# Layer 1's first feed-forward matrix by seven block products instead of eight, in chunks 2 to 7

## The chip, the cores and the metric

The kernel runs on one core of a Trainium2 chip. The metric is the device time of one execution in microseconds: 1711.4 us before the change (median of three runs, 1711.36 to 1712.46). Engines: PE = TensorE matmul, PEld = its weight load, DVE = VectorE, ACT = ScalarE, POOL = GpSimd, SP = SyncE, which issues nearly all DMAs here.

## The reference

Two trunk layers over 640 tokens (512 latent, 128 context) of width 1024; each is a mixer (attention and convolution) and then a feed-forward part. Only that of layer 1, the last one, is touched:

```
def trunk_layer(x, cvec, lw, layer, ctx):
    ...
    h = rmsnorm(x, lw['g_ff']) * (1.0 + sc2) + sh2
    x = x + g2 * (jnp.square(jax.nn.relu(h @ lw['w_ff1'])) @ lw['w_ff2'])
    return x, new_ctx
```

`w_ff1` is 1024 x 4096 and `w_ff2` 4096 x 1024, all float32. After the last layer comes a final RMS norm.

## The kernel before

Activations lie transposed: features on the 128 partitions, the 640 tokens along the free dimension. So `h` is 8 tiles of 128 x 640, and the hidden layer is 32 tiles of 128 x 640, worked on in 8 chunks of 4 tiles. The token range is cut in two, `HALF = ((0, 384), (384, 640))`, so that a piece fits one PSUM bank of 512 columns. There are eight banks, used in turn (`g()`).

Every float32 operand is kept as a high part (rounded by a cast to fp32r on ScalarE) and a low part (source minus high part): `split`. A product is then three matmuls, high x high, high x low, low x high (`mm3`, lines 245 to 247), accumulated in one bank. For weights the low part is computed by GpSimd, with a few exceptions in the mixer.

Weights arrive in granules of 128 x 1024 float32 (512 KB) by DMA on SP's queue into three raw buffers (`w_dma`), are split in blocks of 512 columns into one of four slots (`w_cut`, `split`), and a slot is free again when the last matmul that reads it is done (`w_done`). One granule of `w_ff1` is one hidden tile (8 k-tiles of 128 x 128); one of `w_ff2` is 512 rows x 256 columns (4 k-tiles, two output tiles).

`ff(l)` is the loop. Chunk 0 is started together with the norm (`ff1_start`). Then for chunk c = 1 to 7 and q = 0 to 3: `ff1(c, q)` makes hidden tile q of chunk c (48 matmuls: 24 of 384 columns, 24 of 256), and `ff2(c - 1, q)` adds two output tiles' share of the chunk before (again 24 and 24). `ff2_end` does the last chunk's second matrix. After each `ff1` half, `ff1_after` makes the hidden values: relu (ACT, from PSUM), square to the high part (ACT), square on DVE, low part by a subtraction on DVE. After each `ff2` piece, `resid` adds it to `x` on DVE. In layer 0 the same loop also runs background jobs (`bg`); in layer 1 it has none.

A scheduler puts each engine's instructions in an order by program order, a priority and its own estimate of when each is ready; within an engine they then run strictly in that order. The hidden tiles live in two buffers that alternate by chunk (`hid`). The memory of the mixer's tiles (`e`, `mla`, `c`, `rope`, `edge`) is part of the arena `fa` for the whole program.

Of the kernel before, what the change touches and what calls it, by code (L numbers as in the profile page):

```python
# [9 lines left out]
F32 = mybir.dt.float32  # L10
# [24 lines left out]
def _addresses(sizes, base=0):  # L35
# [42 lines left out]
KINDS = ("D", "D")  # L78
ROWS = (1,1,0,0)
END = object()  # L80
PROGRAM = "Sa0 ma0 | T2 ev2 xa0 Sb0 mb0 xb0 sc1 | PV3 oc3 |".split()


class Builder:
    def __init__(self, tc, sb, ps, d):
        self.tc, self.nc, self.d = tc, tc.nc, d
        self.fa = sb.tile([128, F_SIZE // 4], F32, name="fa")
        self.ra = sb.tile([128, R_SIZE // 4], F32R, name="ra")
        self.gb = [ps.tile([128, 512], F32, name=f"g{i}") for i in range(2)]
# [24 lines left out]
        self.right = self.squares = None  # L114
        self.last_square = False
        self.w_split = self.w_load = 0
        self.ng = L * NGRAN

    def _view(self, arena, at, shape):
        n = int(np.prod(shape))  # L120
# [5 lines left out]
        return v  # L126

    def F(self, name, off, *shape):
        return self._view(self.fa, F_AT[name] + off, shape)

    def R(self, name, off, *shape):
# [84 lines left out]
            self.w_load += 1  # L216

    def w_cut(self):
        while self.w_split < min(self.w_load, self.ng):
            n = self.w_split  # L220
            i = self.w_slot(n)
            if self.held[i] or (i > 1 and self.we is None):
                return
            self.held[i] = True
            raw = self.w_raw(n)
            hi, lo = self.w_hl(n)
            for j, s in enumerate((slice(0, 512), slice(512, 1024))):
                self.split(hi[:, s], lo[:, s], raw[:, s], self.nc.vector if n < 4 and CUT[n * 2 + j] == "D" or n > 3 and j and i > 1 and n % NGRAN < NMIX + 4 else None)
            self.w_split += 1
            self.w_dma()  # L230

    def w_get(self, c):
        n = self.w_n
# [918 lines left out]
    def ff2_piece(self, l, c, wv, m, mm, h):  # L1152
        t0, t1 = HALF[h]
        ps = self.g()
        for k in range(4):
            hi, lo = self.hid(c, k)
            cols = slice(mm * 128, mm * 128 + 128)
            self.mm3(ps[:, 0:t1 - t0], (wv[0][:, k, cols], wv[1][:, k, cols]), (hi[:, t0:t1], lo[:, t0:t1]), k == 0, k == 3)
        return ps

    def ff2(self, l, c, q):
        wv = self.w_get(256)
        for h in range(2):
            for mm in range(2):
                m = 2 * q + mm
                ps = self.ff2_piece(l, c, wv, m, mm, h)
                if h == 1 and mm == 1:
                    self.w_done()
                self.resid(l, G2, m, h, ps)
            self.tick(1200)  # L1170

    def ff2_end(self, l, c, chain):
        ws = [self.w_get(256) for _ in range(4)]
        for h in range(2):
            for q in range(4):
                for mm in range(2):
                    m = 2 * q + mm
                    ps = self.ff2_piece(l, c, ws[q], m, mm, h)
                    if h == 1 and mm == 1:
                        self.w_done()  # L1180
# [25 lines left out]
    def start(self):  # L1206
# [123 lines left out]
        for _ in range(3):  # L1330
            self.w_dma()
        self.chain(self.mod_rows(0, (G1, SC2, SH2, G2)))
        nc.sync.dma_start(self.F("rope", 0, 1152), d["cst"][:, 0:1152])
# [145 lines left out]
    def ff(self, l):  # L1479
        nc = self.nc  # L1480
        self.ring = self.banks
        self.junk = self.F("e", 0, 1024)
        ring = [self.F("e", 4096, 1024), self.F("e", 8192, 1024), self.F("mla", 0, 1024)]
        self.bg = []
        self.ff1_start(l)
        if l + 1 < L:
            self.bg = self.mod_jobs(l + 1, range(6), ring, BGP[4])
        for c in range(1, 8):
# [5 lines left out]
        self.norm_at("mla", 6144)  # L1494
        if l + 1 < L:
            self.mod_gain(l + 1, 0)
            self.lead = self.norm(l + 1, 0, 0)
# [48 lines left out]
    def run(self):  # L1546
        with (self.tc.manual_schedule(engines={getattr(mybir.EngineType, e) for e in MAN}) if MAN else contextlib.nullcontext()):
            self.o_tile("s", F32)
            self.swap("s", "we")
            for l in range(L):  # L1550
                with self.tc.tile_pool(name=f"at{l}", bufs=1) as pool:
                    self.at = pool.tile([128, A_SIZE // 4], F32, name=f"at{l}")
                    self.mix(l)
                with self.tc.tile_pool(name=f"hd{l}", bufs=1) as pool:
                    self.hd = pool.tile([128, 4480], F32R, name=f"hd{l}")
                    self.ff(l)
            self.right.__exit__(None, None, None)
            self.under.__exit__(None, None, None)
# [45 lines left out]
def _layout(a):  # L1604
# [5 lines left out]
    for l in range(L):  # L1610
# [103 lines left out]
```

## Time and profile before

| | us |
|---|---|
| median of 3 runs | 1711.4 |
| the profiled execution, whole | 1712.74 |
| its span, first to last instruction | 1710.7 |
| PE busy / DVE / ACT / POOL | 1633.3 / 1051.2 / 728.2 / 659.3 |

The profiled execution is 1.3 us over the median; 2.0 us of it lie outside the span. Times below are microseconds from the span's start. In layer 1's feed-forward the granules follow one another every 7.03 us: chunk 1 starts at 1278.2, chunk 2 at 1334.4, `ff2_end` at 1671.9.

### The profile page before, as it was taken

The numbers are of one execution on the slowest core, as the hardware profiler recorded it, in microseconds if no ns is written. First come the engines' busy times: TensorE is split into PE (matmuls) and PEld (weight loads), VectorE is DVE, ScalarE is ACT, GpSimd is POOL, SyncE is SP. The second block draws the span as 40 slices with busy tenths as digits, with TensorE's granted clock in tenths as the row PEclk, the third lists the DMA queues.
The fourth block names the chain that finished last, engine by engine and source line by source line (L and its number), as shares of the span: only waits on it lengthen the run. The fifth ranks groups of instructions, "written<-read, shape, count | busy, mean of one in ns | idle before, by whom it ended". The sixth has DMA issues, their size and how long they took to land. (4 is left out here: it accounts for less than half of the span.)

```text
span 1710.7 us, 29286 instructions
## 1 busy us (share of the span) xinstructions
PE 1633.3 (95%) x11416; PEld 1531.2 (90%) x11416; DVE 1051.2 (61%) x2064; ACT 728.2 (43%) x1617; POOL 659.3 (39%) x527
## 2 busy tenths in 40 slices
PE   7989999999899999999999899999999999999997
PEld 4867988878899999999999888887789999999997
DVE  4791438867788787885377943886773333333335
ACT  4322576755622222233343257676553323332222
POOL 0242543414444444544324364341443333333330
PEclk7998999999999999999999999999999999999999
DMA  9465333302244454443222233330112222222221
GB/s 358 157 227 173 100 101 98 88 21 79 71 151 157 151 159 152 157 150 99 75 71 72 65 95 101 86 87 21 50 57 92 74 75 75 75 74 75 75 62 62
DMA packets 62330, 178.27 MB, mean 104 GB/s; under 512 B 8656, under 2 KB 20048, under 8 KB 62192
## 3 DMA queue, kind: packets, MB, share of 16 engines
q1 hardware_dynamic: 61984, 176.14, 33.7%
q8 instruction: 89, 1.46, 0.4%
q14 instruction: 49, 0.40, 0.1%
q0 software_dynamic: 64, 0.14, 0.0%
q10 hardware_dynamic: 144, 0.13, 0.0%
HBM read 158.52 MB, written 3.83 MB: 95 GB/s over the span
## 5 line engine op out<-in xcount | busy, mean ns | idle before, releaser
L194 POOL TENSOR_TENSOR ra<-fa,ra 128x512 fp32r<-128x512 f32 (+1 forms) x239 | 353.4, 1494 | 501.8 <-ACT ra L193 481.9
L194 POOL TENSOR_TENSOR we<-fa,we 128x512 fp32r<-128x512 f32 x126 | 185.7, 1485 | 261.3 <-ACT we L193 239.6
L1098 DVE TENSOR_TENSOR fr<-fr 128x384 f32<-128x384 f32 (+1 forms) x128 | 102.2, 800 | 281.5 <-ACT or L1097 153.5
L193 ACT CAST ra<-fa 128x512 fp32r<-128x512 f32 (+1 forms) x240 | 147.2, 622 | 252.7 <-PE s L246 152.7
L245 PE MATMUL s<-ra 128*128 128x256 f32 (+2 forms) x704 | 218.7, 311 | 2.4 <-DVE fa L1386 2.1
L246 PE MATMUL s<-ra 128*128 128x256 f32 (+2 forms) x704 | 217.8, 309 | 0.0
L247 PE MATMUL s<-ra 128*128 128x256 f32 (+2 forms) x704 | 217.4, 309 | 0.0
L393 DVE SCALAR_TENSOR_TENSOR fa<-s,fa 128x128 f32<-128x128 f32 (+1 forms) x312 | 121.9, 427 | 73.8 <-PE s L247 73.7
L193 ACT CAST we<-fa 128x512 fp32r<-128x512 f32 x132 | 81.5, 620 | 180.5 <-PE s L246 132.2
L302 DVE CUSTOM_DVE_ANT_0 fa<-fa 128x1024 f32<-128x1024 f32 x96 | 153.4, 1598 | 0.1
L245 PEld LDWEIGHTS s<-ra 128*128 128x128 f32 x704 | 134.2, 191 | 8.4 <-issue 4.0
L393 DVE SCALAR_TENSOR_TENSOR fa<-g,fa 128x128 f32<-128x128 f32 (+1 forms) x264 | 109.2, 443 | 44.5 <-PE g L247 43.8
L246 PEld LDWEIGHTS s<-ra 128*128 128x128 f32 x704 | 134.1, 190 | 2.4 <-issue 2.3
L247 PEld LDWEIGHTS s<-ra 128*128 128x128 f32 x704 | 134.0, 190 | 0.2 <-issue 0.2
L247 PE MATMUL g<-ra 128*128 128x256 f32 (+2 forms) x404 | 123.7, 306 | 9.1 <-POOL ra L194 9.1
L245 PE MATMUL g<-ra 128*128 128x256 f32 (+2 forms) x404 | 128.1, 317 | 0.7 <-ACT fa L656 0.4
L424 DVE SCALAR_TENSOR_TENSOR fa<-fa 128x670 f32<-128x670 f32 x120 | 127.0, 1123 | 0.4
L246 PE MATMUL g<-ra 128*128 128x256 f32 (+2 forms) x404 | 123.4, 306 | 0.0
L245 PE MATMUL g<-or,ra 128*128 128x384 f32 (+1 forms) x328 | 112.8, 344 | 4.8 <-DVE or L194 4.4
L246 PE MATMUL s<-ra,we 128*128 128x256 f32 (+1 forms) x360 | 112.2, 312 | 4.6 <-DVE ra L371 4.6
L245 PE MATMUL s<-ra,we 128*128 128x256 f32 (+1 forms) x360 | 110.6, 309 | 4.2 <-DVE fa L393 2.3
L247 PE MATMUL s<-ra,we 128*128 128x256 f32 (+1 forms) x360 | 110.5, 307 | 0.0
(294 smaller groups left out, 4425.1 us busy)
## 6 DMA issues: line engine op xcount, KB each, us to landing
fa<-in_wg SPq DMA_DIRECT2D x187, 512.0 KB, 3.7
fa<-in_wmod SPq DMA_DIRECT2D x68, 512.0 KB, 4.3
at<-in_wmod SPq DMA_DIRECT2D x25, 512.0 KB, 7.2
ra<-ra SPq DMA_DIRECT2D x64, 96.0 KB, 2.5
ra<-ra SPq DMA_DIRECT2D x64, 80.0 KB, 2.8
fa<-in_nab SPq DMA_DIRECT2D x24, 192.0 KB, 4.0
fa<-in_xT SPq DMA_DIRECT2D x8, 320.0 KB, 6.7
os<-in_wmod SPq DMA_DIRECT2D x3, 512.0 KB, 10.2
```

The costliest lines, as they stand in the source:

```text
L193: nc.scalar.copy(hi, src)
L194: (lo_eng or nc.gpsimd).tensor_tensor(out=lo, in0=src, in1=hi.bitcast(F32), op=ALU.subtract)
L245: nc.tensor.matmul(out, a[0], b[0], start=start, stop=False)
L246: nc.tensor.matmul(out, a[0], b[1], start=False, stop=False)
L247: nc.tensor.matmul(out, a[1], b[0], start=False, stop=stop)
L302: self.nc.vector.tensor_tensor_reduce(out=self.junk, in0=slot, in1=self.cb[:, v], scale=1.0, scalar=0.0, op0=ALU.mult, op1=ALU.add, accum_ ...
L393: self.mark = nc.vector.scalar_tensor_tensor(out=xs, in0=ps[:, a - t0:b - t0], scalar=self.mod(l, v, which)[:, m:m + 1], in1=xs, op0=ALU.m ...
L424: nc.vector.scalar_tensor_tensor(out=y, in0=g[:, j:j + 670], scalar=dwh[:, c, j:j + 1], in1=y, op0=ALU.mult, op1=ALU.add)
L1098: nc.vector.tensor_tensor(out=r, in0=r, in1=r, op=ALU.mult)
```

## The change

For chunks 2 to 7 of layer 1, two hidden tiles are made at a time (`ff1_pair`). Their matrix product, 256 outputs by 1024 inputs by 640 tokens, is cut in two by two blocks: two output tiles, two halves of the inputs (4 k-tiles each), two halves of the tokens (`TH` = 320). Instead of eight block products seven are made (Strassen's method in Winograd's form), each of 4 k-tiles x 3 = 12 matmuls of 320 columns. Some of the seven take sums of blocks as operands, and their results are combined by additions:

- weights: `unit_jobs` makes three sums and one difference of 512 columns per pair on DVE, in `ts` or in place in the raw buffers; seven blocks are split instead of four. Two raw granules are taken up together, and their buffers go back together, after the seventh block.
- tokens: `t_jobs` makes T1, T2, T3 (in the new tile `tt`), each in 4 k-tiles, high and low part, as background jobs in chunk 1, and T4 in place of the quarter of `h` that is used no more, after the last `ff1` of chunk 1. They are used by all 12 pairs.
- results: one copy on ACT and seven additions on DVE per pair, each from a PSUM bank and an SBUF buffer; then relu, square and low part on 320 columns, four times (`hid_out`).

The four slots become eight units of one 512-column block each (`unit`, `unit_cut`, `unit_done`); second-matrix granules take two units. From chunk 2 on the order is: pair, `ff2`, `ff2`, pair, `ff2`, `ff2`. To make room, the mixer's tiles move to an arena of their own (`fm`), which is given back before the feed-forward of layer 1.

```
@@ class Builder
+WINO = NGRAN * (L - 1) + NMIX + 12
+TH = T // 2
...
     def w_cut(self):
+        if self.jobs:
+            self.unit_cut()
         while self.w_split < min(self.w_load, self.ng):
             n = self.w_split
+            if n >= WINO:
+                return self.unit_cut()
...
+    def unit_jobs(self, n):
...
+        a11, a12, a21, a22 = raw[:, 0:512], raw[:, 512:1024], nxt[:, 0:512], nxt[:, 512:1024]
+        s3, s2 = self.ts[:, 0:512], self.ts[:, 512:1024]
...
+        def sums():
+            sub(s3, a11, a21)
+            sub(a21, a21, a22, ALU.add)
+            return sub(s2, a21, a11)
+
+        def both():
+            self.w_dma()
+            self.w_dma()
+        return [lambda: a11, sums, lambda: a12, lambda: s3, lambda: a21, lambda: a22, lambda: sub(a12, a12, s2), both]
+
+    def unit_cut(self):
+        while True:
...
+            u = self.un % 8
+            if self.busy[u] or self.held[u // 2]:
+                return
+            src = self.jobs.pop(0)()
+            hi, lo = self.unit(u)
+            self.split(hi, lo, src)
...
+    def t_jobs(self):
...
+        def t1(k):
+            x, y = part(0, 1, k), part(0, 0, k)
+            hold[k] = combine((x[0], y[0]), (x[1], ALU.add), (y[1], ALU.subtract))
+            put(0, k, hold[k])
+
+        def t2(k):
+            x = part(1, 1, k)
+            put(1, k, combine((x[0], hold[k]), (x[1], ALU.add)))
+
+        def t3(k):
+            x, y = part(1, 1, k), part(0, 1, k)
+            put(2, k, combine((x[0], y[0]), (x[1], ALU.add), (y[1], ALU.subtract)))
+
+        def t4(k):
+            x, y = part(1, 0, k), [a[:, k].bitcast(F32) for a in self.t_view(1)]
+            put(3, k, combine((x[0], y[0]), (x[1], ALU.add), (y[1], ALU.subtract)))
+        return [(1500, lambda f=f, k=k: f(k), 0) for k in range(4) for f in (t1, t2, t3)], [lambda k=k: t4(k) for k in range(4)]
...
+    def ff1_pair(self, c, m):
...
+        nc.scalar.copy(s1, product(self.quarter(0, 0)))
+        add(u2, product(self.t_view(1)), s1)
+        result(product(self.quarter(1, 0)), s1, m, 0)
+        add(u3, product(self.t_view(2)), u2)
+        p5 = product(self.t_view(0))
+        result(p5, u3, m + 1, 1)
+        add(u4, p5, u2)
+        result(product(self.quarter(0, 1)), u3, m + 1, 0)
+        result(product(self.quarter(1, 1)), u4, m, 1)
...
     def ff(self, l):
...
+        if last:
+            self.bg, fourth = self.t_jobs()
         for c in range(1, 8):
             for q in range(4):
+                if last and c > 1:
+                    if q % 2 == 0:
+                        self.ff1_pair(c, q)
+                        self.ff2(l, c - 1, q)
+                        self.ff2(l, c - 1, q + 1)
+                    continue
                 self.ff1(c, q)
+                if last and q == 3:
+                    self.drain()
+                    for job in fourth:
+                        job()
                 self.ff2(l, c - 1, q)
```

How the change moves instructions, at the two places that matter below. First DVE, at the end of chunk 1. Before (L1098 and L1099 make the low part of a hidden tile, L393 adds an output piece to `x`):

```order
L1098 TENSOR_TENSOR fr_10931<-fr_10931 128x384
L1099 TENSOR_TENSOR or<-fr_10931,or 128x384
L1098 TENSOR_TENSOR fr_10931<-fr_10931 128x256
L1099 TENSOR_TENSOR or<-fr_10931,or 128x256
L393 SCALAR_TENSOR_TENSOR fa<-s_65,fa 128x384
L393 SCALAR_TENSOR_TENSOR fa<-s_66,fa 128x384
L393 SCALAR_TENSOR_TENSOR fa<-s_67,fa 128x128 x2
L393 SCALAR_TENSOR_TENSOR fa<-g_63,fa 128x128 x2
```

Now, in the same place on DVE (L1259 and L1261 combine T sums, L201 is the low part of a split: written to `tt` for T1 to T3, to `ra` for T4; L465 is `resid`; L1313 the first addition of the first pair):

```order
L201 TENSOR_TENSOR tt_10997<-fa,tt_10997 128x320
L1261 TENSOR_TENSOR fa<-fa,tt_10997 128x320
L1259 TENSOR_TENSOR fa<-ra,tt_10997 128x320
L465 SCALAR_TENSOR_TENSOR fa<-s_70,fa 128x384
L201 TENSOR_TENSOR ra<-fa,ra 128x320
L1261 TENSOR_TENSOR fa<-fa,ra 128x320
L465 SCALAR_TENSOR_TENSOR fa<-s_71,fa 128x128
L1261 TENSOR_TENSOR fa<-fa,tt_10997 128x320
L465 SCALAR_TENSOR_TENSOR fa<-s_71,fa 128x128
L465 SCALAR_TENSOR_TENSOR fa<-g_67,fa 128x128 x2
L201 TENSOR_TENSOR ra<-fa,ra 128x320
L1313 TENSOR_TENSOR fa<-s_69,fa 128x320
```

The T sums stand between the residual additions of chunk 1's last `ff2`, and the low part of T4's last k-tile is the last of them, just ahead of the first pair's additions.

Second ACT, at the start of chunk 2. Before (L193 is the cast of a weight block, L1096 and L1097 the relu and square of hidden tile 3 of chunk 1 and of tile 0 of chunk 2):

```order
L193 CAST ra<-fa 128x512 x2
L1096 ACTIVATE fr_10931<-s_67 128x256
L1097 ACTIVATE or<-fr_10931 128x256
L193 CAST ra<-fa 128x512 x2
L1096 ACTIVATE fr_10931<-g_64 128x384
L1097 ACTIVATE hd_10991<-fr_10931 128x384
```

Now (L200 is the cast of a split: 512 columns are a weight unit, 320 columns a T tile, in `tt` T3, in `ra` T4; L1168 and L1169 are the relu and square, L1323 the copy of the first product):

```order
L1168 ACTIVATE fr_10935<-s_71 128x256
L1169 ACTIVATE or<-fr_10935 128x256
L200 CAST ra<-fa 128x320
L200 CAST tt_10997<-fa 128x320
L200 CAST ra<-fa 128x512
L200 CAST ra<-fa 128x320
L200 CAST ra<-fa 128x512
L200 CAST we_10933<-fa 128x512
L200 CAST ra<-fa 128x320
L1323 COPY fa<-g_68 128x320
```

The last three casts of T4 now stand among the casts of the weight units, and each of these waits for PE to leave the unit.

## Rows read from the trace of the kernel before

**Rows 1.** The page: busy time, share of span and instructions of each engine.

```profile
PE 1633.3 (95%) x11416; PEld 1531.2 (90%) x11416; DVE 1051.2 (61%) x2064; ACT 728.2 (43%) x1617; POOL 659.3 (39%) x527
```

**Rows 2.** Windows: busy us (instructions) of each engine, granted clock; chunks 1, 2, 7.

```profile
1278.18:1334.40 56.22, 56.22 (x386) 56.22 (x385) 22.14 (x43) 18.58 (x38) 22.46 (x18) 1.00 0.28 88
1334.40:1390.66 56.26, 56.26 (x386) 56.26 (x385) 19.15 (x41) 16.80 (x33) 20.67 (x17) 1.00 0.25 76
...
1615.70:1671.90 56.20, 56.20 (x386) 56.20 (x385) 19.11 (x40) 16.74 (x33) 20.61 (x17) 1.00 0.20 57
```

**Rows 3.** Timeline of PE: start, length, engine, line; one granule of `w_ff1`.

```profile
1404.44 0.34 PE L245 MATMUL s<-ra 128*128 128x384 f32 x1
...
1408.61 0.28 PE L245 MATMUL g<-ra 128*128 128x256 f32 x1
...
1411.48 0.34 PE L245 MATMUL g<-hd,ra 128*128 128x384 f32 x1
```

**Rows 4.** Timeline of PE, at 172 us: matmuls of 288 columns.

```profile
171.77 0.29 PE L246 MATMUL s<-ra 128*128 128x288 f32 x1
...
172.30 0.30 PE L247 MATMUL s<-ra 128*128 128x288 f32 x1
```

**Rows 5.** Groups by form, 1300 to 1690 us: busy us, mean ns, idle before.

```profile
L393 DVE SCALAR_TENSOR_TENSOR fa<-s,fa 128x384 f32<-128x384 f32 x46 | 28.3, 615 | 22.4 <-PE s L247 22.4
L393 DVE SCALAR_TENSOR_TENSOR fa<-s,fa 128x128 f32<-128x128 f32 x80 | 24.4, 347 | 32.8 <-PE s L247 32.8
L1099 DVE TENSOR_TENSOR or<-fr,or 128x384 fp32r<-128x384 f32 x14 | 7.8, 557 | 0.5
L1099 DVE TENSOR_TENSOR or<-fr,or 128x256 fp32r<-128x256 f32 x15 | 6.4, 427 | 0.5
L193 ACT CAST we<-fa 128x512 fp32r<-128x512 f32 x52 | 32.3, 620 | 80.5 <-PE s L246 79.1
L1096 ACT ACTIVATE fr<-s 128x384 f32<-128x384 f32 x20 | 9.8, 492 | 72.2 <-PE s L247 72.2
L1097 ACT ACTIVATE or<-fr 128x384 fp32r<-128x384 f32 x14 | 7.3, 524 | 0.4
L194 POOL TENSOR_TENSOR we<-fa,we 128x512 fp32r<-128x512 f32 x52 | 67.2, 1303 | 115.5 <-ACT we L193 113.9
```

**Rows 6.** Groups by form, whole span: a 512-column subtraction on DVE.

```profile
L194 DVE TENSOR_TENSOR wes<-fa,wes 128x512 fp32r<-128x512 f32 x4 | 2.5, 684 | 0.0
```

**Rows 7.** Timeline of DVE and POOL at 1278 to 1285 us.

```profile
1278.17 3.95 POOL L194 TENSOR_TENSOR ra<-fa,ra 128x512 fp32r<-128x512 f32 x3 [1.50 <-ACT ra L193]
...
1279.76 1.23 DVE L1098 TENSOR_TENSOR fr<-fr 128x256 f32<-128x256 f32 x1 [2.34 <-ACT hd L1097]
...
1281.02 1.39 DVE L1099 TENSOR_TENSOR hd<-fr,hd 128x256 fp32r<-128x256 f32 x1
1282.33 0.41 DVE L1098 TENSOR_TENSOR fr<-fr 128x256 f32<-128x256 f32 x1
...
1283.58 0.56 DVE L1098 TENSOR_TENSOR fr<-fr 128x384 f32<-128x384 f32 x1 [0.38 <-ACT or L1097]
1284.17 0.56 DVE L1099 TENSOR_TENSOR or<-fr,or 128x384 fp32r<-128x384 f32 x1
```

**Rows 8.** Windows of 2 us: PE busy first, the granted clock third from last.

```profile
1250.00:1252.00 2.00, 0.54 (x4) 0.22 (x2) 2.00 (x3) 0.62 (x2) 1.92 (x3) 0.97 0.36 80
1252.00:1254.00 2.00, 1.83 (x5) 1.65 (x6) 0.53 (x1) 0.55 (x2) 0.11 (x1) 0.50 0.46 182
1254.00:1256.00 2.00, 2.00 (x9) 1.75 (x7) 0.00 (x0) 1.63 (x2) 0.00 (x0) 0.68 0.00 0
1256.00:1258.00 2.00, 1.95 (x12) 1.83 (x12) 0.96 (x3) 1.69 (x5) 0.00 (x0) 1.00 0.00 0
```

**Rows 9.** DMA issues of the weights, from the page: KB each, median us to landing.

```profile
fa<-in_wg SPq DMA_DIRECT2D x187, 512.0 KB, 3.7
```

**Rows 10.** Waits of PE: us in total, times, longest.

```profile
PE s L1375 <- DMA at<-in_wmod: 5.8, 2, 4.4
PE s L1375 <- DMA fa<-in_wmod: 2.1, 1, 2.1
```

More of the change, by code (lines that the diff above doesn't have):

```diff
@@ L117, in __init__ @@
         self.ng = L * NGRAN
+        self.jobs, self.un, self.busy, self.units = [], 2 * self.w_slot(WINO), [False] * 8, []
     def _view(self, arena, at, shape):
@@ L128, in F @@
     def F(self, name, off, *shape):
+        if name in M_AT:
+            return self._view(self.fm, M_AT[name] + off, shape)
         return self._view(self.fa, F_AT[name] + off, shape)
@@ L230, in w_cut, with unit, sub, unit_done @@
             self.w_dma()
+    def unit(self, u):
+        hi, lo = (self.R("w", 0, 2048), self.R("w", 8192, 2048)) if u < 4 else (self.we[:, 0:4096], self.we[:, 1024:4096])
+        at = (u % 4) * 512 if u < 4 else (u % 4) // 2 * 2048 + u % 2 * 512
+        return hi[:, at:at + 512], lo[:, at:at + 512]
+    def unit_jobs(self, n):
+        nc = self.nc
+        raw = self.w_raw(n)
+        first = (n - WINO) % 4 == 0 and n < L * NGRAN - 4
+        if not first:
+            self.w_split += 1
+            return [lambda: raw[:, 0:512], lambda: raw[:, 512:1024], self.w_dma]
+        self.w_split += 2
+        nxt = self.w_raw(n + 1)
+        a11, a12, a21, a22 = raw[:, 0:512], raw[:, 512:1024], nxt[:, 0:512], nxt[:, 512:1024]
+        s3, s2 = self.ts[:, 0:512], self.ts[:, 512:1024]
+        def sub(out, x, y, op=ALU.subtract):
+            nc.vector.tensor_tensor(out=out, in0=x, in1=y, op=op)
+            return out
+        def sums():
[8 more added lines that the diff above has]
+        while True:
+            if not self.jobs:
+                n = self.w_split
+                if n >= self.ng or n + (2 if (n - WINO) % 4 == 0 and n < L * NGRAN - 4 else 1) > self.w_load:
+                    return
+                self.jobs = self.unit_jobs(n)
+            u = self.un % 8
+            if self.busy[u] or self.held[u // 2]:
+                return
+            src = self.jobs.pop(0)()
+            hi, lo = self.unit(u)
+            self.split(hi, lo, src)
+            self.busy[u] = True
+            self.units.append(u)
+            self.un += 1
+            if len(self.jobs) == 1:
+                self.jobs.pop(0)()
+    def unit_done(self, *us):
+        for u in us:
+            self.busy[u] = False
+        self.w_cut()
+    def unit_get(self, n):
+        us, self.units = self.units[:n], self.units[n:]
+        assert len(us) == n
+        return us
     def w_get(self, c):
@@ L1157, in ff2_piece @@
             cols = slice(mm * 128, mm * 128 + 128)
-            self.mm3(ps[:, 0:t1 - t0], (wv[0][:, k, cols], wv[1][:, k, cols]), (hi[:, t0:t1], lo[:, t0:t1]), k == 0, k == 3)
-        return ps
+            if isinstance(wv, list):
+                w = [a[:, k % 2 * 256:k % 2 * 256 + 256][:, cols] for a in self.unit(wv[k // 2])]
+            else:
+                w = [a[:, k, cols] for a in wv]
+            self.mm3(ps[:, 0:t1 - t0], w, (hi[:, t0:t1], lo[:, t0:t1]), k == 0, k == 3)
+        return ps
@@ new lines, in ff2_get, with ff2_done, quarter, t_view @@
+    def ff2_get(self, l, c):
+        return self.unit_get(2) if l == L - 1 and c else self.w_get(256)
+    def ff2_done(self, wv):
+        if isinstance(wv, list):
+            self.unit_done(*wv)
+        else:
+            self.w_done()
+    def quarter(self, i, j):
+        k, t = slice(4 * i, 4 * i + 4), slice(TH * j, TH * j + TH)
+        return self.hh[:, k, t], self.hl[:, k, t]
+    def t_view(self, i):
+        return tuple(self._view(self.tt, 10240 * i + o, (4, TH)) for o in (0, 5120))
@@ new lines, in t_jobs, with combine, put, part @@
+    def t_jobs(self):
+        nc = self.nc
+        def combine(first, *rest):
+            t = self.tmp(TH)
+            nc.vector.tensor_tensor(out=t, in0=first[0], in1=first[1], op=ALU.subtract)
+            for x, op in rest:
+                nc.vector.tensor_tensor(out=t, in0=t, in1=x, op=op)
+            return t
+        def put(i, k, t):
+            hi, lo = (a[:, k] for a in (self.t_view(i) if i < 3 else self.quarter(0, 1)))
+            self.split(hi, lo, t, nc.vector)
+        def part(i, j, k):
+            return [a[:, k].bitcast(F32) for a in self.quarter(i, j)]
+        hold = {}
+        def t1(k):
[12 more added lines that the diff above has]
+        return [(1500, lambda f=f, k=k: f(k), 0) for k in range(4) for f in (t1, t2, t3)], [lambda k=k: t4(k) for k in range(4)]
@@ L1172, in ff2_end @@
     def ff2_end(self, l, c, chain):
-        ws = [self.w_get(256) for _ in range(4)]
+        ws = [self.ff2_get(l, c) for _ in range(4)]
         for h in range(2):
@@ L1493, in ff @@
         self.table(TABLE_LN)
[L1494 removed]
+        self.norm_at("mla" if l + 1 < L else "conv", 6144 if l + 1 < L else 0)
         if l + 1 < L:
```

63 lines of the change are left out of this document (50 added, 13 removed).

## The prediction

> **What bounds the kernel now.** I read the busy line of the page first: PE works 95% of the span, no other engine over 61% [rows 1]. An average hides stages, so next the windows of layer 1's feed-forward. Chunks 1 to 7 each take 56.2 to 56.3 us, and in all of them PE is busy for the whole window at full granted clock, while DVE has about 19 us of work, ACT 17, POOL 21 [rows 2]. So here, and only where PE never waits, a matmul saved is time saved. The third view is the timeline of PE, because the recorded length of a matmul (0.34 and 0.28 us) overlaps the next one: what counts is the distance between starts. In one granule 24 matmuls of 384 columns go from 1404.44 to 1408.61 (173.8 ns each) and 24 of 256 to 1411.48 (119.6 ns) [rows 3]. A line through both gives 0.423 ns per column and 11 ns per matmul. It says 133 ns for 288 columns; the trace has four such starts in 0.53 us, 132.5 ns [rows 4].
>
> **The saving on PE.** 320 columns are halfway between 256 and 384: 146.7 ns. A pair of hidden tiles took 48 x 173.8 + 48 x 119.6 = 14.08 us; it takes 7 x 12 = 84 x 146.7 = 12.32 us. Saved: 1.76 us a pair. Six chunks of two pairs: 12 x 1.76 = 21.1 us. The `ff2` matmuls keep number and size. Bounds for 320 columns, which no row shows: 119.6 and 173.8 ns; I take the line, since the 288-column row lies on it.
>
> **What each pair adds, and what hides it.** A pair and its two `ff2` granules will be a cycle of 12.3 + 14.1 = 26.4 us of PE.
> POOL: 7 weight blocks and 4 of `ff2` instead of 8: 11 x 1.30 = 14.3 us [rows 5].
> ACT: 11 casts at 0.62, four relus and squares on 320 columns at about 0.44 and 0.47 (between the 256 and 384 rows' sizes), a copy at 0.44: 10.9 us [rows 5].
> DVE: operations with both inputs in SBUF cost 427 ns at 256 columns and 557 at 384 [rows 5], so 492 at 320. Eight for the hidden tiles are 3.9 us; four weight sums at 0.684 are 2.7 [rows 6]; seven additions from PSUM, between 347 (128 columns) and 615 (384), at about 0.55 are 3.8; the residual additions stay at 4 x 0.615 + 8 x 0.347 = 5.2 [rows 5]. Sum 15.6 us.
> Each is under 26.4, so none sets the pace by its amount. By latency: a unit is split after its reader eight units earlier is done. The tightest are the seventh product's (freed as the pair begins, wanted 6 x 1.76 = 10.6 us later) and the second half of the first `ff2` granule (freed at 1.8, wanted at 12.3). A split is a DVE difference, a cast and POOL's subtraction, 0.7 + 0.6 + 1.3 = 2.6 us: some 8 us to spare. Two raw buffers now come free together and their loads are late by a few us, landing 3.7 us after issue [rows 9]: inside that margin. PSUM banks come round after eight pieces, at the least 10 us. So the steady state I cost at nothing; without this margin each late unit would stop PE by what it lacks.
>
> **DVE in chunk 1: where it is not hidden.** T1 to T4 are 60 operations on 320 columns: per k-tile 3 + 1, 2 + 1, 3 + 1 and 3 + 1. The sixth product of the first pair reads T4, and its last k-tile is wanted at 1334.4 + 5 x 1.76 + 9 x 0.147 = 1344.5. DVE can begin when the first hidden tile of chunk 1 is through, at 1284.7 [rows 7]: a window of 59.8 us. Up to the last T4 row DVE has, by the order shown with the change: 60 x 0.52 (0.49 and the 0.03 between starts [rows 7]) = 31.2; four weight sums 2.8; the low parts of four hidden tiles (2.1 each), less the one pair of operations that is through by then, 7.2; four granules of residual additions 4 x 2.6 = 10.4 (rows that overlap in part, so at most this; I take 9.8). Sum 51.0 us. That fits, were DVE alone.
>
> It is not alone. While POOL runs a row of subtractions, a DVE operation on two SBUF inputs that takes 0.41 us beside an idle POOL takes 1.23 and 1.39 us, ending just after a POOL operation [rows 7]: some 0.9 us lost to each POOL operation met. In the window POOL has about 18 (two per granule, then one per product). DVE's time is 41.2 / 51.0 = 0.8 in such operations: 18 x 0.8 x 0.9 = 13 us. 51.0 + 13.0 = 64.0, so T4 is 4.2 us late and PE stands for that long, in pieces. The Trainium skill, "SBUF — State Buffer", section "Who interferes with whom", says that a DVE instruction with two SBUF inputs and a GpSimd instruction that reads SBUF exclude one another, and that the second to issue blocks until the first is done. The trace agrees in kind (1.23 and 1.39 against 0.41 us); taken in full, 18 x 1.3 = 23 us, it would make T4 some 14 us late instead of 4.2.
>
> After an idle gap PE's clock also falls: at 1250 us PE stands for 1.5 of 2 us, and the granted clock is then 0.50 and 0.68 in the next two windows (1.2 GHz, then part of each) before it is 1.00 again [rows 8]. That loses 1.0 + 0.6, so about 1.5 us. Stall and clock together: 6 us, once. Bounds: none if POOL's operations fall where DVE waits anyway; about 17 if every one is met in full and the casts of T4, which now stand behind casts that wait for PE to leave a unit, hold DVE up as well. I take 6, from the rows nearest to it. The residual additions and the first pair's additions queue behind T4 on DVE; their banks are wanted some 10 us after, so a lag of 5 us stays hidden, and with 15.6 us of own work per 26.4 it is worked off in a pair or two.
>
> **The rest.** In the first 165 us the scheduler swaps some loads of the modulation weights with granule loads on SP's queue, and a few matmuls. PE waits there 7.9 us for such loads [rows 10]; a shift of one matmul group or one load may move that by 2 us either way; I take nothing. The end (`ff2_end`, norm) has the same work; its units come free as the slots did.
>
> **Sum.** From the profiled execution: 1712.7 - 21.1 + 6 = 1697.6. The median lies 1.3 lower: 1696 us.
>
> **Rivals.**
> A, no stall: POOL and DVE interleave better, T4 is in time: 1711.4 - 21.1 = 1690. For it: the sum without contention fits. Against: DVE is near full for four granules in a row, and strictly in order.
> B, T4 much later: 14 us and the clock, or a second stall at the next pair because the sums of its weights queue behind T4 on DVE: 1711.4 - 21.1 + 15.5 = 1706. The full exclusion above is this case. Against: each blocked operation in the rows still got through with under 1 us lost.
> C, slower: DVE and POOL take turns in the steady state. If all of DVE's work in a cycle excluded POOL's, 15.6 + 14.3 = 29.9 us would be the cycle, against 28.2 us before: 12 x 1.7 = 20 us on top, 1732. It decides from where the turns need more than 26.4 us, and the kernel is slower from 28.2. Against: over half of DVE's 15.6 us reads PSUM, and those rows keep their 615 ns in a stretch where POOL works a third of the time [rows 2, 5]; only 6.6 + 14.3 = 20.9 us exclude one another.
> D, 320 columns cost as 384: 84 x 173.8 = 14.6 us a pair, 0.5 more than before: with the stall 1723. Against: 288 columns do not cost as 384 [rows 4].
>
> **How the numbers follow.** The forecast (stall and clock 3 to 11 us: 1693 to 1701) 0.52; A 0.24; B 0.13; C 0.06; D 0.01; something else that cancels the gain 0.04. The range holds the forecast, A with 2 us gained at the start, and most of B: 1688 to 1705. A measurement of this kernel can tell 0.2%, 3.4 us, from no change. Faster by more than that: forecast, A and most of B, 0.88; within it: the end of B and half of the cancelling case, 0.04; slower: C, D and the other half with some of the unknown, 0.08.
>
> **What would show it.** Right: from the second pair on cycles of 26.4 us with PE busy throughout, 84 matmuls of 320 columns 147 ns apart, and one stretch of idle PE of about 4 us ahead of the sixth product of the first pair, waiting for a DVE subtraction into `ra`, with a lower clock behind it. DVE busy nearly all of chunk 1, many of its 320-column operations over 1 us. Wrong: 320-column starts over 160 ns apart; PE waiting in every cycle for POOL's or ACT's weight units; or waits in chunk 1 itself, because the lagging residual additions hold the banks.

## The result, and the profile after

The changed kernel takes 1720.7 us (median of 4 runs, 1718.9 to 1723.3) against 1711.4 of before: a ratio of 1.0057, 95% interval 1.0040 to 1.0075. It is slower, where 1696 was forecast with a range of 1688 to 1705. The profiled execution took 1723.28 us, with a span of 1721.2.

The busy line of the page, which answers to [rows 1]:

```profile
PE 1624.7 (94%) x11272; PEld 1519.0 (88%) x11272; DVE 1169.5 (68%) x2256; ACT 753.4 (44%) x1681; POOL 716.0 (42%) x563
```

There are 144 matmuls fewer, as counted, and PE is busy 8.6 us less, yet the span is 10.5 us longer: PE waits where it did not before. Next come the matmuls themselves. This is the timeline of PE at the start of a pair, answering to [rows 3]:

```profile
1484.31 0.31 PE L317 MATMUL s<-ra 128*128 128x320 f32 x1
1484.46 0.31 PE L318 MATMUL s<-ra 128*128 128x320 f32 x1
1484.61 0.31 PE L319 MATMUL s<-ra 128*128 128x320 f32 x1
```

They start 0.15 us apart; twelve of them take 1.76 us, so 146.7 ns each, the value worked out. The saving is there whenever PE runs. The windows of chunks 2, 4 and 7 (columns as in [rows 2]):

```profile
1340.50:1396.90 56.40, 53.78 (x363) 52.70 (x361) 38.88 (x73) 20.77 (x43) 31.63 (x22) 1.00 0.25 75
...
1453.70:1515.00 61.30, 56.18 (x363) 55.54 (x362) 33.23 (x62) 20.41 (x41) 29.32 (x22) 0.94 0.23 69
...
1628.50:1682.50 54.00, 53.34 (x363) 52.81 (x362) 30.67 (x58) 20.54 (x41) 29.46 (x22) 1.00 0.25 79
```

A chunk was to take 52.8 us. It takes 54.0 to 61.3, and in chunk 4 the granted clock is 0.94. A cycle is a pair with its two `ff2` granules, read from the first 320-column matmul of one pair to that of the next. The eleven cycles are 28.8, 27.7, 27.7, 29.2, 30.6, 30.7, 29.4, 29.1, 27.6, 27.5, 27.6 us and not 26.4. Chunk 1, which has only the sums T1 to T4 added, takes 63.0 us (1277.51 to 1340.48) and not 56.2. What PE waits for from 1270 to 1715 us (us in total, times, longest), where before had 1.9 us of waits in all:

```profile
PE s L317 <- DVE fa L465: 7.3, 6, 2.5
PE s L317 <- DVE fr L1313: 6.5, 3, 2.6
PE s L317 <- DVE fa L1313: 4.4, 8, 1.0
PE s L317 <- ACT fr L1168: 3.4, 1, 3.4
```

No weight unit stands here. L1313 (additions of the products), L465 (residual additions) and L1168 (the relu of a hidden tile of chunk 1) read PSUM: PE waits for a bank. Here is the longest wait of chunk 4 on the timeline of PE, and the 2-us windows around it (clock third from last, as in [rows 8]):

```profile
1500.62 0.34 PE L319 MATMUL s<-or,ra 128*128 128x384 f32 x1
1503.59 0.58 PE L317 MATMUL s<-or,ra 128*128 128x256 f32 x1 [2.63 <-DVE fr L1313]
1503.97 0.42 PE L318 MATMUL s<-or,ra 128*128 128x256 f32 x1
1504.19 0.42 PE L319 MATMUL s<-or,ra 128*128 128x256 f32 x1
```

```profile
1502.00:1504.00 2.00, 0.41 (x2) 0.41 (x3) 2.00 (x6) 0.43 (x1) 0.00 (x0) 0.84 0.00 0
1504.00:1506.00 2.00, 2.00 (x11) 2.00 (x11) 1.85 (x4) 0.52 (x2) 0.00 (x0) 0.50 0.00 0
1506.00:1508.00 2.00, 2.00 (x16) 2.00 (x16) 0.73 (x3) 0.62 (x1) 0.00 (x0) 0.81 0.00 0
```

PE stands 2.6 us, and then runs at a granted clock of 0.50 (1.2 GHz) for two more; matmuls of 256 columns start 0.21 us apart instead of 0.12. What it waits for is the addition of the seventh product, whose matmuls PE had issued by 1496.6, before the two `ff2` pieces that end at 1500.8: the result that holds PE up was made three pieces earlier, not eight. The timeline of DVE shows why the addition came so late:

```profile
1491.92 1.35 DVE L262 TENSOR_TENSOR ts<-fa 128x512 f32<-128x512 f32 x1 [1.64 <-DMA fa<-in_wg]
1493.20 1.58 DVE L1296 TENSOR_TENSOR fr<-fr 128x320 f32<-128x320 f32 x1
1494.70 0.48 DVE L1313 TENSOR_TENSOR fa<-s,fa 128x320 f32<-128x320 f32 x1
...
1498.92 0.49 DVE L1296 TENSOR_TENSOR fr<-fr 128x320 f32<-128x320 f32 x1 [0.82 <-ACT hd L1295]
1500.59 1.74 DVE L262 TENSOR_TENSOR fa<-fa,ts 128x512 f32<-128x512 f32 x1 [1.18 <-POOL ra L201]
...
1503.06 0.48 DVE L1313 TENSOR_TENSOR fr<-s,fa 128x320 f32<-128x320 f32 x1
```

DVE takes its work in order. It stood 1.64 us for the transfer of the raw weights, then 1.18 us at a12 - s2 for POOL's reading of a12, which that sum overwrites, and the addition for PE was queued behind. Three operations on the way (1.35, 1.58 and 1.74 us) also took longer than such operations take elsewhere in this cycle (0.69 us for 512 columns, 0.49 for 320), together by 2.8 us, as much as the two waits. The chain of waits of this stretch, in order of time (start, us, what), ends in the same way:

```profile
1498.97 1.60 POOL ra L201
1500.57 0.02 issue
1500.59 1.74 DVE fa L262
1502.33 0.40 DVE hx L1297
1502.73 0.06 DVE fr L1296
1502.79 0.27 issue
1503.06 0.49 DVE fr L1313
1503.55 0.04 issue
1503.59 0.58 PE s L317
```

Over the ten cycles from 1369.25 to 1656.09 us (groups by form, as in [rows 5]):

```profile
L1296 DVE TENSOR_TENSOR fr<-fr 128x320 f32<-128x320 f32 x40 | 30.4, 760 | 10.2 <-ACT or L1295 5.0 <-ACT hd L1295 4.1
L262 DVE TENSOR_TENSOR ts<-fa 128x512 f32<-128x512 f32 x20 | 17.6, 882 | 17.7 <-DMA fa<-in_wg 17.3
L262 DVE TENSOR_TENSOR fa<-fa,ts 128x512 f32<-128x512 f32 x10 | 17.6, 1762 | 11.8 <-POOL we L201 7.1 <-POOL ra L201 4.7
```

One 512-column sum in each cycle takes 1762 ns, against the 684 of [rows 6], and the sums wait 17.3 us for transfers and 11.8 for POOL.

Why three pieces? The eight places for a result are six halves of the three two-bank tiles `s` and the two tiles `g`, in the order g0, g1, s0a, s1a, s2a, s0b, s1b, s2b. The wait above fits a program in which the first matmul into a half waits for the last reading of the other half of its tile too: a piece in s0b waits for the reader of the piece in s0a, three earlier. **Theory (halves):** the tiles leave a slack of two pieces, 4.2 us when both have 384 columns, and DVE is later than that. On the timelines its addition of the seventh product starts 5.9 to 6.7 us after PE has left that product, in each of the cycles 2 to 11. **Rival (turns):** rival C of the prediction, DVE and POOL excluding one another until a cycle doesn't hold both. A third candidate are the sums T1 to T4, from whose lag DVE might never recover.

### The profile page after: what moved, and what is told of

It reads as the page before. It is cut to its first block, busy times and chain, and to the rows that moved or that the text cites. A ratio compares the mean times of both kernels' runs of the same rounds, so it can differ in the third digit from the quotient of the medians.

```text
span 1721.2 us, 29442 instructions
## 1 busy us (share of the span) xinstructions
PE 1624.7 (94%) x11272; PEld 1519.0 (88%) x11272; DVE 1169.5 (68%) x2256; ACT 753.4 (44%) x1681; POOL 716.0 (42%) x563
## 5 line engine op out<-in xcount | busy, mean ns | idle before, releaser
L201 POOL TENSOR_TENSOR ra<-fa,ra 128x512 fp32r<-128x512 f32 x241 | 362.7, 1521 | 461.2 <-ACT ra L200 412.4
L201 POOL TENSOR_TENSOR we<-fa,we 128x512 fp32r<-128x512 f32 x134 | 200.3, 1509 | 219.3 <-ACT we L200 164.1
L200 ACT CAST ra<-fa 128x512 fp32r<-128x512 f32 x246 | 148.7, 617 | 233.3 <-PE s L318 153.4
L317 PE MATMUL s<-ra 128*128 128x256 f32 (+3 forms) x644 | 198.9, 309 | 1.2 <-DVE fa L1313 1.0
L318 PE MATMUL s<-ra 128*128 128x256 f32 (+3 forms) x644 | 197.6, 307 | 0.1
L319 PE MATMUL s<-ra 128*128 128x256 f32 (+3 forms) x644 | 197.4, 306 | 0.0
L465 DVE SCALAR_TENSOR_TENSOR fa<-s,fa 128x128 f32<-128x128 f32 (+1 forms) x316 | 122.3, 425 | 58.8 <-PE s L319 58.5
L200 ACT CAST we<-fa 128x512 fp32r<-128x512 f32 x140 | 85.7, 619 | 156.3 <-PE s L318 82.5
L374 DVE CUSTOM_DVE_ANT_0 fm<-fm 128x1024 f32<-128x1024 f32 x96 | 151.6, 1579 | 0.1
L1170 DVE TENSOR_TENSOR fr<-fr 128x384 f32<-128x384 f32 (+1 forms) x80 | 66.7, 838 | 104.7 <-ACT or L1169 54.1
L465 DVE SCALAR_TENSOR_TENSOR fa<-g,fa 128x128 f32<-128x128 f32 (+1 forms) x260 | 107.5, 443 | 39.4 <-PE g L319 38.6
L317 PEld LDWEIGHTS s<-ra 128*128 128x128 f32 x644 | 122.3, 190 | 9.4 <-issue 4.8
L318 PEld LDWEIGHTS s<-ra 128*128 128x128 f32 x644 | 122.4, 190 | 1.0 <-issue 0.7
L319 PEld LDWEIGHTS s<-ra 128*128 128x128 f32 x644 | 122.3, 190 | 0.2 <-issue 0.2
L319 PE MATMUL g<-ra 128*128 128x256 f32 (+3 forms) x364 | 112.7, 310 | 9.1 <-POOL ra L201 9.1
L317 PE MATMUL g<-ra 128*128 128x256 f32 (+3 forms) x364 | 116.7, 321 | 0.7 <-ACT fm L728 0.4
L317 PE MATMUL g<-or,ra 128*128 128x384 f32 (+1 forms) x316 | 111.0, 351 | 4.6 <-DVE or L201 4.2
L318 PE MATMUL g<-ra 128*128 128x256 f32 (+3 forms) x364 | 112.3, 308 | 0.0
L318 PE MATMUL g<-or,ra 128*128 128x384 f32 (+1 forms) x316 | 101.3, 321 | 1.4 <-POOL or L201 1.4
L319 PE MATMUL g<-or,ra 128*128 128x384 f32 (+1 forms) x316 | 101.8, 322 | 0.0
L765 ACT COPY at<-s 128x640 f32<-128x640 f32 (+2 forms) x120 | 65.8, 549 | 57.0 <-PE s L759 55.2
```

The lines of the kernel that those rows point to most:

```text
L200: nc.scalar.copy(hi, src)
L201: (lo_eng or nc.gpsimd).tensor_tensor(out=lo, in0=src, in1=hi.bitcast(F32), op=ALU.subtract)
L317: nc.tensor.matmul(out, a[0], b[0], start=start, stop=False)
L318: nc.tensor.matmul(out, a[0], b[1], start=False, stop=False)
L319: nc.tensor.matmul(out, a[1], b[0], start=False, stop=stop)
L374: self.nc.vector.tensor_tensor_reduce(out=self.junk, in0=slot, in1=self.cb[:, v], scale=1.0, scalar=0.0, op0=ALU.mult, op1=ALU.add, accum_ ...
```

## The experiments

The stretch ahead of chunk 1 differs by up to 11 us from run to run (PE is free for chunk 1 at 1267.3 to 1278.3 us in the traces), so two measures are given: the ratio to the kernel before on the same chip, and from the one trace of each run the time from PE being free for chunk 1 to the end of chunk 7. That is 393.9 us in before (1277.85 to 1671.71 by the starts of matmuls); 393.9 - 21.1 = 372.8 would be the saving alone, and 378.8 the forecast with its 6 us. The last column is the lag: how long after PE has left the seventh product DVE starts its addition, in the cycles 2 to 11.

| | ratio, 95% interval | chunks 1 to 7, us | cycles 2 to 11, us | lag, us |
|---|---|---|---|---|
| changed kernel | 1.0057 (1.0040-1.0075) | 405.0 | 27.5-30.7 | 5.9-6.7 |
| e1 single banks | 0.9937 (0.9916-0.9958) | 381.4 | 26.4 | 6.3-7.2 |
| e2 other order of halves | 1.0029 (1.0011-1.0047) | 397.6 | 27.4-28.3 | 6.2-6.8 |
| e3 fourth raw buffer, own a12 - s2 | 0.9948 (0.9928-0.9968) | 386.4 | 26.4, once 27.3 and 29.0 | 1.1-1.4 |
| e4 e1 and e3 | 0.9894 (0.9880-0.9909) | 378.2 | 26.4 | 1.2-4.7 |
| e6 without the sums T | one run, 1707.9 | 396.9 | 27.7-30.8 | 5.9-6.5 |
| e7 without POOL's low parts | one run, 1690.4 | 374.1 | 26.4 | 0.4-1.0 |
| e8 before, single banks | 1.0013 (0.9998-1.0028) | | | |
| e9 e4, products 6 and 7 swapped | 0.9894 (0.9870-0.9917) | 377.0 | 26.4 | 3.2-3.8 |
| e10 own a12 - s2 alone | 1.0012 (0.9993-1.0031) | 402.4 | 26.9-30.6 | 5.3-5.7 |
| e11 fourth raw buffer alone | 0.9997 (0.9980-1.0014) | 397.9 | 26.6-30.4 | 4.9-5.0 |

**e1: eight tiles of one bank.** From chunk 1 of layer 1 on, nothing else changed.

```
+        if l == L - 1:
+            self.single_banks()
...
+        self.ring = self.banks = [ps.tile([128, 512], F32, name=f"f{i}")[:, 0:512] for i in range(8)]
```

> The changed kernel, but from chunk 1 of layer 1 on the eight PSUM banks are eight tiles of one bank each, instead of two of one bank and three of two. Theory 'halves': in the changed kernel a piece waits until DVE has read the other half of its two-bank tile, three pieces back, so PE has two pieces (3 to 4 us) of slack and not seven; DVE falls 4 to 7 us behind in each pair. With single banks the waits in chunks 2 to 7 go: cycles of 26.4 to 26.7 us, chunks 2 to 7 in 316 to 321 us instead of 342, in all 1690 to 1701 us. Rival 'turns': DVE and POOL exclude each other so much that DVE's work does not fit a cycle; then it falls behind without end, cycles stay at 27.5 us or more, 1712 to 1722 us.

1695.4 us. The ten cycles in one window, PE busy throughout, and DVE's groups in it:

```profile
1369.44:1633.30 263.86, 263.86 (x1802) 263.86 (x1801) 163.77 (x313) 99.62 (x201) 150.56 (x111) 1.00 0.27 81
```

```profile
L262 DVE TENSOR_TENSOR ts<-fa 128x512 f32<-128x512 f32 x20 | 18.6, 928 | 18.6 <-DMA fa<-in_wg 16.5 <-POOL ra L201 1.7
L262 DVE TENSOR_TENSOR fa<-fa,ts 128x512 f32<-128x512 f32 x10 | 17.7, 1767 | 11.8 <-POOL we L201 7.1 <-POOL ra L201 4.7
```

DVE is as busy and as late as in the changed kernel, 1767 ns and 16.5 and 11.8 us of waits and a lag of 6.3 to 7.2 us, but PE no longer waits at all in these cycles. So the turns do not set the cycle (rival C falls); the tile's halves turn DVE's lag into PE's.

**e2: the halves four pieces apart.**

```
+            b = self.banks
+            self.ring = self.banks = [b[0], b[2], b[3], b[4], b[1], b[5], b[6], b[7]]
```

> The changed kernel with another order of the same banks from chunk 1 on, in which the two halves of a tile are four pieces apart instead of three. 'Halves': one piece more of slack, 1.4 to 2.1 us of each wait go where PE waits once per cycle: 1703 to 1714 us. 'Turns': no change, 1719 to 1722 us.

1712.9 us. The worst cycles go (30.7 to 28.3), but every one now loses 1.1 to 1.9 us, with one wait each. Three pieces after the seventh product are two of 384 columns and one of 256, 5.6 us; a lag of 6.2 to 6.8 us and the 0.5 us of the addition are longer.

**e3: DVE in time.** Two-bank tiles stay. There is a fourth raw buffer, a12 - s2 is written to its own buffer and made earlier, when the third block is split, and the raw buffers are given back a block earlier.

```
-        return [lambda: a11, sums, lambda: a12, ..., lambda: a22, lambda: sub(a12, a12, s2), both]
+        return [lambda: a11, sums, third, ..., lambda: a22, both, lambda: s4]
...
+                        self.raw4 = pool.tile([128, 1024], F32, name=f"rx{l}")
```

> The changed kernel with a fourth raw weight buffer, the difference of the seventh block in a buffer of its own (made when the third block is split), and both raw buffers of a pair given back after the sixth block instead of the seventh. Takes away what DVE waits for in each pair: the weights' DMA (1.7 us) and POOL's read of the third block (1.2 us). 'Halves': DVE is 3 us less behind, so most waits of PE in chunks 2 to 7 go, those at the end of chunk 1 (7 us) stay: 1698 to 1712 us. 'Turns': the amounts of work are the same, 1716 to 1722 us.

1697.5 us, eight of ten cycles at 26.4. Yet DVE is busier than in the changed kernel (181.2 us in its ten cycles against 163.9), and the wait for transfers is nearly as long as there (15.3 us against 17.3). Groups from 1357.3 to 1621.2 us, and DVE in a cycle that begins at 1412.69:

```profile
L1304 DVE TENSOR_TENSOR or<-fr,or 128x320 fp32r<-128x320 f32 x20 | 21.5, 1076 | 0.0
...
L265 DVE TENSOR_TENSOR ts<-rx,fa 128x512 f32<-128x512 f32 x10 | 12.6, 1261 | 0.0
L265 DVE TENSOR_TENSOR ts<-fa,ts 128x512 f32<-128x512 f32 x10 | 12.0, 1201 | 0.0
...
L265 DVE TENSOR_TENSOR ts<-fa,rx 128x512 f32<-128x512 f32 x10 | 7.3, 734 | 15.3 <-DMA rx<-in_wg 15.3
```

```profile
1415.51 1.26 DVE L265 TENSOR_TENSOR ts<-fa,ts 128x512 f32<-128x512 f32 x1
1416.70 0.48 DVE L1320 TENSOR_TENSOR fa<-s,fa 128x320 f32<-128x320 f32 x1
...
1426.26 0.48 DVE L1320 TENSOR_TENSOR fr<-s,fa 128x320 f32<-128x320 f32 x1
```

The low parts of the hidden tiles (`or`) take 1076 ns, against about 0.48 us beside an idle POOL, and there is hardly any loss. What has changed is the place of the weight sums. Here the last of the four (1415.51) is done before the pair's first addition (1416.70), in each of the ten cycles; in the changed kernel all four stand between the first and the seventh addition. So what DVE loses at the weight sums, by waiting and by longer operations, falls where no addition of the pair is queued behind it, and the seventh comes 1.1 to 1.4 us after its product. The cycle of 29.0 us is the one in which DVE stood longest for a transfer, 2.9 us at the start of the pair; PE then waited 2.4 us for a residual addition. In the cycle of 27.3 us PE waited 0.6 us for a weight unit, as it never did in the changed kernel.

**e10, e11: which of the two waits.** One half of e3 in each.

```
e10:
-        return [..., lambda: sub(a12, a12, s2), both]
+        return [..., lambda: sub(s4, a12, s2), both]
e11:
+        if n >= self.n4:
+            i = (n - self.n4) % 4
+            return self.F("raw", 4096 * ((self.n4 + i - 1) % 3), 1024) if i else self.raw4
```

> The changed kernel (two-bank tiles, three raw buffers) with one thing of the run with the fourth raw buffer: the block a12-s2 is written into a buffer of its own, at its old place, so VectorE no longer has to wait for GpSimd's reading of a12 (11 waits, 13.0 us in the changed kernel), and raw buffers are given back one reader earlier. In-order theory: what VectorE's additions stand behind is any wait of its weight sums; these 13 us go and the 18.6 us of waits for the weights' transfers remain, so about half of the lag goes: cycles of 26.9 to 28.0 us, time 1705 to 1713. If GpSimd is the one that counts: cycles near 26.4 to 26.8 and the time at the 1697 of the run with both. If the transfers are: no change, within 3 us of 1721.

> The changed kernel with the other thing alone: a fourth raw buffer for the weights, a12-s2 still written over a12. In-order theory: the 18.6 us of waits for the weights' transfers go, or most of them, and the 13.0 us behind GpSimd remain: cycles of 26.9 to 28.0 us, 1705 to 1713 us. If the transfers are the one that counts: cycles near 26.4 to 26.8, the time at 1697. If GpSimd is: within 3 us of 1721 (in the run with both, VectorE still waited 15.3 us for transfers, which speaks for this one).

By themselves they take 402.4 and 397.9 us: 2.6 and 7.1 less than the changed kernel, and e3, which has both and makes a12 - s2 earlier, 18.6 less. DVE's wait for POOL ahead of a12 - s2 is gone in both runs, and the waits for transfers are 17.0 us in e10 and 8.7 in e11, against 17.3. The weight sums still stand between the additions, in e11 the fourth close ahead of the seventh addition, with no wait in front of it (the product ended at 1491.1):

```profile
1493.95 0.68 DVE L265 TENSOR_TENSOR fa<-fa,ts 128x512 f32<-128x512 f32 x1
1494.55 1.57 DVE L1299 TENSOR_TENSOR fr<-fr 128x320 f32<-128x320 f32 x1
1496.04 0.48 DVE L1316 TENSOR_TENSOR fr<-s,fa 128x320 f32<-128x320 f32 x1
```

The lag is 5.3 to 5.7 and 4.9 to 5.0 us, still more than two pieces, and the middle cycles take 27.8 to 30.6 us. e11 has less waiting than e3 (8.7 us against 15.3) and loses more, so the amount of waiting alone is not what decides; the traces point to the place of the sums in DVE's order, which neither half of the edit changes enough. Making a12 - s2 earlier was not tried alone. I had expected cycles of 26.9 to 28.0 us from either half, if both kinds of wait counted alike; both runs have longer ones.

**e6: without T1 to T4.**

```
-            self.bg, fourth = self.t_jobs()
+            self.bg, fourth = [], []
+            for i in range(3):
+                for k in range(4):
+                    for a, b in zip(self.t_view(i), self.quarter(1, 1)):
+                        nc.scalar.copy(a[:, k], b[:, k].bitcast(F32))
```

> The changed kernel without the sums T1 to T4 of the activations: their places in the products hold plain copies of one quarter of h, made by ScalarE ahead of chunk 1, and T4 is not made (its product reads whatever stands in h's place), so the outputs are not the reference's. Halves theory (each piece waits for the reader of the other half of its two-bank tile, two pieces of slack): the twelve cycles of a pair stay as uneven as in the changed kernel, 27.4 to 30.7 us each, since nothing in them depends on the sums once these are made; chunk 1 gets back most of its 7 us, and the first pair's stall before its product with T4 goes; in all some 8 to 12 us off the changed kernel. Sums theory (the sums on VectorE push all its later work late, and it never catches up): the cycles fall to about 26.4 us and the whole time to 1695 or below.

The cycles 2 to 11 stay at 27.7 to 30.8 us; chunk 1 falls from 63.0 to 56.6 us. The third candidate falls: the sums cost once, in chunk 1 and the first pair, and are 8 of the 32 us that the changed kernel loses.

**e7: without POOL's subtraction for the low part of the units.**

```
-            self.split(hi, lo, src)
+            self.nc.scalar.copy(hi, src)
```

> The changed kernel without the low parts of the weight units of chunks 2 to 7: GpSimd's subtraction for each block is left out (ScalarE's cast of the high part stays) and the low matmuls read what stands in the place, so the outputs are not the reference's. Halves theory with VectorE held up by GpSimd: VectorE's two-input sums of the weights and squares go from 1.2 to 1.7 us to about 0.5, raw buffers come back earlier, and with VectorE in time two pieces of slack suffice: cycles of 26.4 to 27.0 us, all in all 10 to 16 us off the changed kernel. If GpSimd's readings are no part of VectorE's lag, the cycles stay at 27.5 to 30.7 us and the time within 3 us of the changed kernel's 1721.

Two-bank tiles and three raw buffers, and yet no cycle over 26.4 us, nor a stall before T4. The window of the changed kernel's ten cycles, and of the same ten here:

```profile
1369.25:1656.09 286.84, 270.81 (x1802) 266.83 (x1801) 163.92 (x310) 100.55 (x201) 149.17 (x110) 0.99 0.24 74
```

```profile
1358.25:1622.12 263.87, 263.87 (x1803) 263.87 (x1801) 139.72 (x310) 105.37 (x200) 0.00 (x0) 1.00 0.27 81
```

```profile
L1296 DVE TENSOR_TENSOR fr<-fr 128x320 f32<-128x320 f32 x40 | 19.5, 488 | 9.3 <-ACT hd L1295 4.1 <-ACT or L1295 4.1
L262 DVE TENSOR_TENSOR ts<-fa 128x512 f32<-128x512 f32 x20 | 13.8, 688 | 3.4 <-DMA fa<-in_wg 3.3
L262 DVE TENSOR_TENSOR fa<-fa,ts 128x512 f32<-128x512 f32 x10 | 6.9, 685 | 0.0
```

Of the 23.0 us between the two windows PE stands 16.0 (286.84 - 270.81); for the other 6.9 it is busy longer with the same work, as with the clock of 0.50 after the stall above. The same 310 instructions of DVE take 139.7 us beside an idle POOL and 163.9 beside a working one. The sum that took 1762 ns takes 685, and the waits of the sums, 17.7 + 11.8 us, are 3.4. The four sums still stand between the additions, but the lag is 0.4 to 1.0 us. POOL is thus the source of DVE's lag by both ways, the longer operations and the waits (for POOL's reading, and for raw buffers that come back late). How much of PE's loss belongs to each way is not separated; in the stretch shown above they were 2.8 us each. The Trainium skill, "SBUF — State Buffer", section "Who interferes with whom", says that a DVE instruction with two SBUF inputs contends with a GpSimd instruction that reads SBUF, that the contention is an exclusive lock, and that the order of issue decides which of the two blocks. 1762 against 685 ns agrees: 1.08 us lost, somewhat less than one POOL operation of 1.3 to 1.4.

**e8: single banks in before**, the control.

```
+        if l == L - 1:
+            self.single_banks()
```

> The kernel before with the same eight single-bank tiles from chunk 1 of layer 1. Halves theory: before has four products a granule and no weight work on VectorE, its waits for PSUM in chunks 2 to 7 are 1.9 us together, so at most those 1.9 us are won and the one-time wait of about 2 us for the old tiles is lost: within 0.2% of before. If single banks were a gain of their own (each piece freed earlier whatever the kernel does), it would be faster by several us, and the comparison of the changed kernel with single banks against before would not tell what the seven products are worth.

1711.9 us, the same within the interval. The two-bank tiles cost nothing in before, where DVE has no weight sums in these chunks.

**e4, e9: the versions that beat both.** e4 has e1's and e3's edits; e9 besides computes the product with T4 last, and gives the raw buffers back after the last block.

```
+        return [lambda: a11, sums, third, lambda: s3, lambda: a21, lambda: s4, lambda: a22, both]
...
+        result(product(self.quarter(1, 1)), u4, m, 1)
         result(product(self.quarter(0, 1)), u3, m + 1, 0)
-        result(product(self.quarter(1, 1)), u4, m, 1)
```

> Both: single banks and the fourth raw buffer. 'Halves': the waits are gone by the first already, so within 3 us of it, 1688 to 1700 us. 'Turns': 1710 to 1722 us.

> Single banks and the fourth raw buffer as in the fastest so far (1689.0), with the sixth and seventh products, and their weight blocks, in the other order, so that the product with T4 is the last of the pair. Theory that what is left in the first cycle is T4 alone (its three pieces stood 3.1 us): T4 has one product (3.5 us) more until it is needed, so the first cycle falls from 29.85 to about 26.4 us and the time by 1 to 3 us, to 1686 to 1688. Rival: ScalarE's cast of the fourth weight block, not T4, is late, or VectorE is only pushed on: the stall moves to another product of the first pair and the time stays within 0.5 us of 1689.0.

e4: 1689.0 us (1688.1 to 1689.8), 1.06% under before. Its first cycle is 29.9 us, with a wait for T4; e9's is 28.6, and the wait is another, for a residual addition behind the sums:

```profile
1340.24 0.38 PE L324 MATMUL f<-ra 128*128 128x320 f32 x1 [1.58 <-DVE fa L472]
```

So swapping gave 1.2 of the 3.5 us that were left, too little to see in the whole time, whose ratios are equal. The stall went to another product, as the rival of my expectation had it; that what remains is DVE's load from chunk 1 is argued from this line, not tried.

## Why the prediction was wrong

**The failed step** is in what hides the additions of each pair: "PSUM banks come round after eight pieces, at the least 10 us. So the steady state I cost at nothing". The banks come round after eight pieces, but three of the eight wait for a reader three pieces back, since they share a tile with it. The slack was two pieces, 4.2 us at most (from 1496.6 to 1500.8 on the timeline), not 10. With single banks, the thing the step assumed, the steady state costs nothing: 26.4 us in each of ten cycles (e1). The term that was put at 0 measured, in the changed kernel, (1682.5 - 1340.5) - 316.6 = 25.4 us in chunks 2 to 7, of which 2.4 are the first cycle's.

**What the step lacked besides:** I counted the late raw buffers against the units' margin only ("inside that margin"), and that held: PE waited for a unit in no cycle. But DVE too waits for raw weights and for POOL's reading, in order, and beside POOL its operations take longer, with additions that PE wants queued behind them. With the weight sums ahead of the pair's additions two pieces suffice in eight of ten cycles (e3), and without POOL's subtractions in all (e7).

**The saving**, 146.7 ns for 320 columns and 1.76 us a pair, was right: PE at 26.4 us a cycle whenever nothing stops it. Rival D falls.

**T1 to T4**, forecast at 6 us once. With single banks the first cycle is 30.9, so 4.5 us over, where I had a stall and clock of 5.7, and the stall stands where it was forecast, at the tenth matmul of the sixth product; it waits first for ACT's cast of T4's last part, which itself stood behind DVE's sum, and then 0.3 us for DVE's subtraction:

```profile
1350.96 0.42 PE L317 MATMUL f<-ra 128*128 128x320 f32 x1 [2.11 <-ACT ra L200]
1351.65 0.42 PE L318 MATMUL f<-ra 128*128 128x320 f32 x1 [0.27 <-DVE ra L201]
```

Chunk 1 takes 57.9 us there from its first matmul, 1.7 more than the 56.2 of before, but that is not the sums: PE stands 2.4 us when it passes to the new tiles, and then runs at a granted clock of 0.50 (1282 to 1284 us), so that the first 24 matmuls take 5.8 us instead of 4.2. In e4, whose clock does not fall there, chunk 1 takes 56.4. In the changed kernel the sums cost more, in another place: chunk 1 grew by 6.8 us and the first cycle by 2.4. "A lag of 5 us stays hidden" rested on the same ten microseconds of slack; instead the lag stopped PE in chunk 1 (3.4 us at once, for a relu that stood on ACT behind a cast of T3), which presumably gave DVE the time that T4 would have lacked (argued, not tried). "[W]aits in chunk 1 itself, because the lagging residual additions hold the banks" was on the list of what would make it wrong.

**Sum.** 1712.7 - 21.1 + 6.8 + 25.4 = 1723.8 against 1723.3 profiled; of the 0.5 left, 0.3 is the earlier start of chunk 1 (1277.51 against 1277.85). Rival C had the sign, but not the mechanism: its 1732 came from exclusion that fills the cycle, and e1 leaves the exclusion in place without a wait of PE. With the tiles as the step assumed them (e1) the time falls by 12.1 us beside its own before (1707.5 to 1695.4), with the raw buffers too (e4) by 18.5, to 1689.0; the forecast said 15.4.

**What stays open:** how much of the lag is waiting and how much longer operations, and which of e3's three edits moves the weight sums ahead of the additions.

## What to carry to other kernels

Read the slack of a ring of PSUM results from the waits that are built, not from the number of banks: a tile of two banks may make one half wait for the reader of the other. When work is put on an engine that also drains PSUM, ask where in its queue the new work will stand and what can hold it up there, not only how busy the engine will be; an engine with 16 us of work in 26 stopped another one here. Where the drain is late, tiles of one bank alone took the cycles to 26.4 us; one more input buffer alone did not.

## What the runs showed of the hardware and the program

The cycles repeat with a period of eight: a pair has 15 pieces (7 products, 8 of `ff2`) on 8 places, so each pair begins one place earlier than the last. Cycles 2 and 3 (27.7, 27.7) and 10 and 11 (27.5, 27.6) are alike, and so are those of e11 (26.7, 26.6 and 26.7, 26.6), while the longest lie between them: cycles 5 and 6 in the changed kernel (30.6, 30.7), 7 and 8 in e11 (30.0, 30.4), at a lag that hardly changes from cycle to cycle. A loss that comes and goes like this points to places in a ring, and not to amounts of work; eleven cycles show the period only once.

The Trainium skill, "PSUM — Partial Sum Buffer", section "PSUM bank collisions raise a hardware error", asks that PSUM be guarded with semaphores by bank and quadrant (32 partitions), or in the simple version by bank. The changed kernel's tiles were guarded by two banks at a time; guarding each by itself (e1) was worth 405.0 - 381.4 = 23.6 us in the same stretch.
